# Stick-breaking attention: one scan of VectorE over two query tiles in place of one scan per tile

## The chip, the cores and the metric

The kernel runs on one core of a Trainium2 chip. The metric is device microseconds of one execution. Five engines work at once and wait for each other by semaphores: TensorE (PE; its weight loads are listed as PEld), VectorE (DVE), ScalarE (ACT), GpSimd (POOL) and SyncE (SP), whose queue issues most DMAs. Each engine runs its instructions in the program's order.

## The reference

A two-layer trunk over 2048 positions of width 1024. Layer 0 is a pooling mixer; layer 1 is attention with 16 heads of width 64. What the change touches is the attention:

```python
logits = einsum('bhtd,bhsd->bhts', q[:, :, t0:L], k[:, :, :L]) * SB_SCALE
mask = s_idx < t_idx
log_keep = where(mask, log_sigmoid(-logits), 0.0)
later = cumsum(log_keep, reverse=True) - log_keep
a = where(mask, exp(log_sigmoid(logits) + later), 0.0)
out = einsum('bhts,bhsd->bhtd', a, v[:, :, :L])
```

For a query t, key s gets beta(t,s) times the product of (1 - beta) over all keys between s and t, with beta the sigmoid of the logit. With p(s) the product of the keeps 1 - beta from key s up to t, the weight is p(s+1) - p(s), so one running product over the keys, from the newest key to the oldest, holds all that is needed. The differences are taken on V instead (rows of V are subtracted ahead of attention), and the product p itself is multiplied with them.

## The kernel before

Queries and keys are cut into 4 chunks of 512. A **slot** is one (query chunk c, head h, key chunk kc); the sweep goes over c = 3, 2, 1, 0, over the 16 heads of each, and over kc from c down to 0, 160 slots in all. A head of c=3 thus has 4 slots, of c=2 three, and so on. The slot with kc = c is the diagonal one, where query tile j (128 queries) sees only the first (j+1)*128 keys of the chunk. A slot has 4 **steps** j, one for each tile of 128 queries, 640 steps in all. In step n three things are issued, each for a different slot:

- `turn` for the slot of 6 steps ago (`LAG_T`): PE transposes one block of 128 keys of all four query tiles of the running product, up to 4 transposes (L981, PSUM tile `psa`, 2 buffers); ACT casts it to fp32r as a high part (L984), DVE subtracts that from it as a low part (L985, tile `at`). The transposes of turn n+2 reuse the PSUM buffer of turn n, so they wait for its subtraction.
- `front` for this step: two matmuls of queries and keys (L956, L957, tile `psl`), ACT's sigmoid of the negative logits, which is the keep (L960, tile `kap`, 4 buffers), and DVE's scan, the running product from the last column to the first (tile `pp`). Off the diagonal (L968) it begins at `carry`, the last value of the same query tile's scan one slot before. On the diagonal (L965) it multiplies and takes the maximum with `ahead`, which is 1 for columns that a query may not see.
- `gather` for the slot of 8 steps ago (`LAG_G`): two matmuls of V with the high and low part (L993, L994).

Between these, PE gets **dense pieces**: single matmuls of 128x512 (L1043, L1045, L1047, tile `psd`) of the gate projection and of what follows attention for the chunk that is done. `shares` spreads them over the steps: it holds a cost of DVE's work in each step (`vector`, by the widths of the scan and of the turned tile), a cost of PE's own work (`tensor`), and gives each step so many pieces that PE's time is in one proportion k to DVE's. From some steps into c=1 on, `turn` is called for two blocks at every even step (turns "by two"), and the pieces are spread evenly.

POOL has the products of the gates (L1083, L1013), the low parts of some operands (L1056, L1128) and 32 DMAs. What a slot's tiles are called and which line issues them does not depend on c.

Of the kernel before, what the change touches and what calls it, by code (L numbers as in the profile page):

```python
# [9 lines left out]
F32 = mybir.dt.float32  # L10
# [5 lines left out]
P = 128  # L16
# [19 lines left out]
def trunk_kernel(ctx, tc, x, xt, pt0, wut, cols, heads, zin, grp, aout, agate, aple,  # L36
# [851 lines left out]
    with ExitStack() as st:  # L888
        kap = st.enter_context(tc.tile_pool(name="kap", bufs=1))
        ppool = st.enter_context(tc.tile_pool(name="ppool", bufs=12))  # L890
        t2 = st.enter_context(tc.tile_pool(name="s2", bufs=2))
# [3 lines left out]

        NK = 4
        kaps = [kap.tile([P, W5], F32, name=f"kap{i}") for i in range(NK)]
        zeros = kap.tile([P, 1], F32, name="zeros")
        V.memset(zeros, 0.0)

        ahead = kap.tile([P, W5], F32, name="ahead")
        G.memset(ahead, 0.0)
        G.affine_select(out=ahead[:, W5 - P :], in_=ahead[:, W5 - P :], pattern=[[-1, P]], compare_op=ALU.is_gt,
                        fill=1.0, base=0, channel_multiplier=1)
        kcount = [0]
# [43 lines left out]
        def front(st, j):  # L949

            w = (j + 1) * P if st["diag"] else W5
            r0 = W5 - w
# [3 lines left out]
            T.matmul(ps[:, :w], qa[:, qs], kk[:, :w], start=True, stop=False)  # L956
            T.matmul(ps[:, :w], qb[:, qs], kk[:, :w], start=False, stop=True)  # L957
            kp = kaps[kcount[0] % NK]
            kcount[0] += 1
            A.activation(out=kp[:, r0:], in_=ps[:, :w], func=AF.Sigmoid, scale=-1.0)  # L960

            def scan():
                pp = ppool.tile([P, W5], F32, tag="pp", name="pp")
                if st["diag"]:
                    V.tensor_tensor_scan(out=pp[:, r0:][:, ::-1], data0=kp[:, r0:][:, ::-1],  # L965
                                         data1=ahead[:, r0:][:, ::-1], initial=1.0, op0=ALU.mult, op1=ALU.max)
                else:
                    V.tensor_tensor_scan(out=pp[:, ::-1], data0=kp[:, ::-1], data1=zeros.to_broadcast([P, W5]),  # L968
                                         initial=st["carry"][j], op0=ALU.mult, op1=ALU.add)
# [124 lines left out]
        def post(c):  # L1094
# [120 lines left out]
        def shares(n0, n1, total):  # L1215
            scan, turned_, gathered = ([widths(n, lag) for n in range(n0, n1)] for lag in (0, LAG_T, LAG_G))
# [3 lines left out]
            tensor = [2 * max(0.109, 0.2265 * a / W5) * (a > 0) + 0.109 * t / P + 2 * max(0.109, 0.2265 * g / W5) * (g > 0)  # L1220
                      for a, t, g in zip(scan, turned_, gathered)]
            part = lambda k: [max(0.5, (k * v - t) / 0.2265) + (AHEAD if n0 + i < LAG_T else 0)
# [138 lines left out]
```

## Time and profile before

| | |
|---|---|
| median of 3 runs | 2652.79 us (2652.48 to 2655.35) |
| the profiled execution | 2653.59 us, its span 2651.8 us |
| granted clock of TensorE | 1.0 |
| busy in the span: PE, PEld, DVE, ACT, POOL | 2640.3, 2205.3, 1984.8, 1427.5, 939.8 us |
| attention, from its first step to the last | about 1305 to 2536 us |
| DVE scans off the diagonal | 384 of 512 columns, mean 1337 ns |
| DVE scans on the diagonal | 64 each of 128, 256, 384, 512 columns |

Rows of a timeline have the start in us from the span's start, the busy time in us, then engine, line, operation, out<-in, shape and, in brackets, idle time of the engine just before with what ended it. Matmuls are pipelined: the next may start before the end that is given for one, so the distance of two starts tells how fast they go. Rows of groups have the count, then the busy time in us and the mean of one in ns, then the idle time before them. In rows of built programs a scan is called SCALAR_TENSOR_TENSOR.

### The profile page before, as it was taken

The numbers are of one execution on the slowest core, as the hardware profiler recorded it, in microseconds if no ns is written. First come the engines' busy times: TensorE is split into PE (matmuls) and PEld (weight loads), VectorE is DVE, ScalarE is ACT, GpSimd is POOL, SyncE is SP. The second block draws the span as 40 slices with busy tenths as digits, with TensorE's granted clock in tenths as the row PEclk, the third lists the DMA queues.
The fourth block names the chain that finished last, engine by engine and source line by source line (L and its number), as shares of the span: only waits on it lengthen the run. The fifth ranks groups of instructions, "written<-read, shape, count | busy, mean of one in ns | idle before, by whom it ended". The sixth has DMA issues, their size and how long they took to land.

```text
span 2651.8 us, 38568 instructions
## 1 busy us (share of the span) xinstructions
PE 2640.3 (100%) x13102; PEld 2205.3 (83%) x13102; DVE 1984.8 (75%) x2570; ACT 1427.5 (54%) x2767; POOL 939.8 (35%) x740
## 2 busy tenths in 40 slices
PE   9999999999999999999999999999999999999999
PEld 8888888888888888888888888888888888888887
DVE  6767835677367763767599999999999998886633
ACT  5446523556136641455466666666666666665531
POOL 2665437644485444753221111122111211212220
PEclk9999999999999999999999999999999999999999
DMA  8658885587856878447787665556766777779865
GB/s 325 227 165 302 283 314 186 191 300 253 308 177 225 301 237 304 147 153 240 229 277 229 187 215 170 175 164 194 209 200 173 190 217 238 201 209 287 248 229 178
DMA packets 469826, 600.40 MB, mean 226 GB/s; under 512 B 28607, under 2 KB 308415, under 8 KB 469629
## 3 DMA queue, kind: packets, MB, share of 16 engines
q1 hardware_dynamic: 463272, 587.39, 67.7%
q0 software_dynamic: 4608, 8.39, 2.0%
q10 hardware_dynamic: 1748, 2.17, 0.3%
q8 instruction: 103, 1.69, 0.3%
q14 instruction: 95, 0.77, 0.1%
HBM read 438.40 MB, written 153.16 MB: 223 GB/s over the span
## 4 chain that ended last, share of the span: by engine, by line
PE 89%; DMA 3%; DVE 2%; POOL 2%; ACT 2%; issue 1%; SPq 0%; ACTq 0%; DVEq 0%; POOLq 0%
PE psd L619 16%; PE psa L981 9%; PE psd L166 8%; PE psd L167 8%; PE psd L168 8%; PE psd L1043 6%; PE psd L1045 6%; PE psd L1047 6%; PE pso L994 5%; PE psl L957 5%; PE pso L993 5%; PE psl L956 5%; DMA wraw<-in_bq_dram 1%; PE psdt L1043 1%; PE psdt L1045 1%
## 5 line engine op out<-in xcount | busy, mean ns | idle before, releaser
L619 PE MATMUL psd<-wpair,x 128*128 128x512 f32 x2304 | 525.6, 390 | 1.4 <-DVE wpair L149 0.8
L968 DVE TENSOR_TENSOR_SCAN pp<-kap,pp,zeros 128x512 f32<-128x512 f32 x384 | 512.7, 1337 | 7.8 <-ACT kap L960 7.1
L984 ACT CAST at<-psa 128x512 fp32r<-128x512 f32 (+3 forms) x640 | 325.7, 523 | 348.8 <-PE psa L981 337.8
L619 PEld LDWEIGHTS psd<-wpair,x 128*128 128x128 f32 x2304 | 431.7, 188 | 93.0 <-DVE wpair L149 2.2
L985 DVE TENSOR_TENSOR at<-psa,at 128x512 fp32r<-128x512 f32 (+3 forms) x640 | 374.9, 598 | 62.2 <-ACT at L984 57.7
L960 ACT ACTIVATE kap<-psl 128x512 f32<-128x512 f32 (+3 forms) x640 | 345.7, 540 | 93.9 <-PE psl L957 90.4
L981 PE MATMUL psa<-ident,pp 128*128 128x128 f32 x2176 | 329.4, 273 | 2.3 <-DVE at L985 1.5
L981 PEld LDWEIGHTS psa<-ident,pp 128*128 128x128 f32 x2176 | 263.7, 141 | 58.4 <-DVE at L985 4.2
L956 PE MATMUL psl<-kk,qa 128*128 128x512 f32 (+3 forms) x640 | 275.1, 430 | 0.2 <-DMA kk<-kd 0.2
L965 DVE TENSOR_TENSOR_SCAN pp<-kap,ahead 128x128 f32<-128x128 f32 (+3 forms) x256 | 224.2, 877 | 40.2 <-ACT kap L960 38.8
L994 PE MATMUL pso<-at,vv 128*128 128x512 f32 (+3 forms) x640 | 234.0, 366 | 0.0
L957 PE MATMUL psl<-kk,qb 128*128 128x512 f32 (+3 forms) x640 | 232.9, 364 | 0.0
L993 PE MATMUL pso<-at,vv 128*128 128x512 f32 (+3 forms) x640 | 232.2, 363 | 0.0
L167 PE MATMUL psd<-xp,wpair 128*128 128x512 f32 x512 | 199.5, 390 | 1.4 <-DVE xp L320 1.4
L166 PE MATMUL psd<-xp,wpair 128*128 128x512 f32 x512 | 200.1, 391 | 0.7 <-ACT xp L319 0.7
L168 PE MATMUL psd<-xp,wpair 128*128 128x512 f32 x512 | 199.3, 390 | 0.0
L149 DVE SCALAR_TENSOR_TENSOR wpair<-wraw,gains,wpair 128x512 fp32r<-128x512 f32 x192 | 164.8, 891 | 31.9 <-ACT wpair L148 30.9
L143 POOL TENSOR_TENSOR wpair<-wraw,wpair 128x512 fp32r<-128x512 f32 x99 | 145.1, 1475 | 78.9 <-ACT wpair L141 72.2
L148 ACT ACTIVATE wpair<-wraw,gains 128x512 fp32r<-128x512 f32 x192 | 129.7, 716 | 47.4 <-DMA wraw<-in_bq_dram 35.6
L1083 POOL TENSOR_TENSOR zr<-zr,sgz 128x512 f32<-128x512 f32 x32 | 61.4, 1919 | 263.8 <-ACT sgz L1082 236.6
L141 ACT CAST wpair<-wraw 128x512 fp32r<-128x512 f32 x148 | 89.1, 618 | 104.5 <-PE psd L168 61.1
L994 PEld LDWEIGHTS pso<-at,vv 128*128 128x128 f32 x640 | 120.3, 188 | 26.4
(206 smaller groups left out, 5400.4 us busy)
## 6 DMA issues: line engine op xcount, KB each, us to landing
kk<-kd SPq DMA_DIRECT2D x160, 256.0 KB
vv<-vd SPq DMA_DIRECT2D x160, 256.0 KB
wraw<-in_kv_dram SPq DMA_DIRECT2D x128, 256.0 KB
wpair<-wzd SPq DMA_DIRECT2D x64, 512.0 KB
wpair<-wod SPq DMA_DIRECT2D x64, 512.0 KB
wpair<-wgd SPq DMA_DIRECT2D x64, 512.0 KB
wpair<-wu SPq DMA_DIRECT2D x48, 512.0 KB
wpair<-wi SPq DMA_DIRECT2D x36, 512.0 KB
```

Source lines behind the costliest of these rows:

```text
L166: T.matmul(ps, wst(units, kt, 0, c0), acts[kt][:, 0], start=(begin and kt == order[0]), stop=False)
L167: T.matmul(ps, wst(units, kt, 0, c0), acts[kt][:, 1], start=False, stop=False)
L168: T.matmul(ps, wst(units, kt, 1, c0), acts[kt][:, 0], start=False, stop=(end and kt == order[-1]))
L619: T.matmul(pss2[i], ck["x2"][kt][:, xh, tk], wst(ws, kt, wh, 0, W5), start=(kt == 0 and xh == 0 and wh == 0), stop=(kt == KT - 1 and wh == 1))
L956: T.matmul(ps[:, :w], qa[:, qs], kk[:, :w], start=True, stop=False)
L957: T.matmul(ps[:, :w], qb[:, qs], kk[:, :w], start=False, stop=True)
L960: A.activation(out=kp[:, r0:], in_=ps[:, :w], func=AF.Sigmoid, scale=-1.0)
L968: V.tensor_tensor_scan(out=pp[:, ::-1], data0=kp[:, ::-1], data1=zeros.to_broadcast([P, W5]), initial=st["carry"][j], op0=ALU.mult, op1=AL ...
L981: T.transpose(pt[:, j * P : (j + 1) * P], pp[:, r0 + kt * P : r0 + (kt + 1) * P], ident)
L985: V.tensor_tensor(out=at[:, 1, cs], in0=pt[:, cs], in1=f(at[:, 0, cs]), op=ALU.subtract)
L993: T.matmul(po[:, cs], vv[:, kt, :], at[:, 0, cs], start=(st["diag"] and kt == 0), stop=False)
L994: T.matmul(po[:, cs], vv[:, kt, :], at[:, 1, cs], start=False, stop=(st["last"] and kt == 3))
```

## The change

Tiles j = 0, 1 and j = 2, 3 of a slot now share one scan. Their keeps stand beside each other in one tile of 1025 columns: the odd tile in columns up to 511, the even one from 513, and column 512 between them holds a keep of 0, so that the product begins anew there from what the second operand has in that column. Off the diagonal the second operand is `entry`, zeros with one column into which POOL copies the odd tile's carry. On the diagonal it is `ahead`, two constant tiles with a 1 in that column. The scan is issued in the odd steps alone. The keeps have 2 buffers in place of 4, the products 5 of 1025 columns in place of 12 of 512. `shares` gets new costs for the scan and the mean width of the two tiles of a pair. A tile `ple` of the dense part moves to another pool.

```diff
+        TWO = 2 * W5 + 1
+        kaps = [kap.tile([P, TWO], F32, name=f"kap{i}") for i in range(2)]
+        entry = kap.tile([P, TWO + W5 + 1], F32, name="entry")
+        firsts = [entry[:, i * (W5 + 1) : i * (W5 + 1) + TWO] for i in range(2)]
+        for t in (*kaps, entry):
+            V.memset(t, 0.0)
+        ahead = []
+        for i in range(2):
+            w = (2 * i + 1) * P
+            d = kap.tile([P, W5 + 1 + w], F32, name=f"ahead{i}")
+            V.memset(d, 0.0)
+            G.memset(d[:, W5 : W5 + 1], 1.0)
+            for at in (W5 - P, W5 + 1 + w - P):
+                G.affine_select(out=d[:, at : at + P], in_=d[:, at : at + P], pattern=[[-1, P]], compare_op=ALU.is_gt,
+                                fill=1.0, base=0, channel_multiplier=1)
+            ahead.append(d)
...
-            kp = kaps[kcount[0] % NK]
-            kcount[0] += 1
-            A.activation(out=kp[:, r0:], in_=ps[:, :w], func=AF.Sigmoid, scale=-1.0)
+            if not j % 2:
+                kcount[0] += 1
+            kp, first = kaps[kcount[0] % 2], firsts[kcount[0] % 2]
+            r0 = W5 - w if j % 2 else W5 + 1
+            A.activation(out=kp[:, r0 : r0 + w], in_=ps[:, :w], func=AF.Sigmoid, scale=-1.0)
+            if not j % 2:
+                if not st["diag"]:
+                    G.tensor_copy(out=first[:, W5 : W5 + 1], in_=st["carry"][j + 1])
+                return lambda: None
             def scan():
-                pp = ppool.tile([P, W5], F32, tag="pp", name="pp")
+                pp = ppool.tile([P, TWO], F32, tag="pp", name="pp")
+                both = slice(r0, W5 + 1 + (w - P if st["diag"] else W5))
                 if st["diag"]:
-                    V.tensor_tensor_scan(out=pp[:, r0:][:, ::-1], data0=kp[:, r0:][:, ::-1],
-                                         data1=ahead[:, r0:][:, ::-1], initial=1.0, op0=ALU.mult, op1=ALU.max)
+                    V.tensor_tensor_scan(out=pp[:, both][:, ::-1], data0=kp[:, both][:, ::-1],
+                                         data1=ahead[j // 2][:, both][:, ::-1], initial=1.0, op0=ALU.mult, op1=ALU.max)
                 else:
-                    V.tensor_tensor_scan(out=pp[:, ::-1], data0=kp[:, ::-1], data1=zeros.to_broadcast([P, W5]),
-                                         initial=st["carry"][j], op0=ALU.mult, op1=ALU.add)
-                st["carry"][j] = pp[:, r0 : r0 + 1]
-                st["a"].append((pp, r0))
+                    V.tensor_tensor_scan(out=pp[:, both][:, ::-1], data0=kp[:, both][:, ::-1], data1=first[:, both][:, ::-1],
+                                         initial=st["carry"][j - 1], op0=ALU.mult, op1=ALU.add)
+                for i, at in ((j - 1, W5 + 1), (j, r0)):
+                    st["carry"][i] = pp[:, at : at + 1]
+                    st["a"].append((pp, at))
...
-                pr = t2.tile([P, 2, W5], F32R, tag="ple", name="ple")
+                pr = pair("ple")
...
-            vector = [(0.15 + 0.0022 * a if a else 0.0) + (0.14 + 0.00105 * t if t else 0.0) for a, t in zip(scan, turned_)]
+            scan = [(widths(n // 2 * 2, 0) + widths(n // 2 * 2 + 1, 0)) / 2 for n in range(n0, n1)]
+            vector = [(0.1 + 0.00208 * a if a else 0.0) + (0.14 + 0.00105 * t if t else 0.0) for a, t in zip(scan, turned_)]
```

What this does to the order of the instructions, first on DVE, at the end of the eleventh head of c=3 and the first steps of the next (the diagonal ones, with `ahead`). Before:

```order
L968 SCALAR_TENSOR_TENSOR pp<-kap_12081,pp,zeros 128x512
L985 TENSOR_TENSOR at<-psa,at 128x512
L968 SCALAR_TENSOR_TENSOR pp<-kap_12082,pp,zeros 128x512
L985 TENSOR_TENSOR at<-psa,at 128x512
L968 SCALAR_TENSOR_TENSOR pp<-kap_12083,pp,zeros 128x512
L985 TENSOR_TENSOR at<-psa,at 128x512
L965 SCALAR_TENSOR_TENSOR pp<-kap_12080,ahead 128x128
```

One subtraction stood between two scans. The same place in the changed program, where the lines of these instructions are L1000, L982 and L979:

```order
L982 SCALAR_TENSOR_TENSOR pp<-kap_12081,pp,entry 128x1025
L1000 TENSOR_TENSOR at<-psa,at 128x512 x2
L982 SCALAR_TENSOR_TENSOR pp<-kap_12080,pp,entry 128x1025
L1000 TENSOR_TENSOR at<-psa,at 128x512 x2
L979 SCALAR_TENSOR_TENSOR pp<-kap_12081,ahead_12086 128x385
```

Now two subtractions stand between two scans, and the first of them stands behind a scan of both tiles. On PE the order of kinds is as before, and only the dense pieces sit elsewhere. The first diagonal steps of that next head, from the matmuls of its 128 keys to the transposes two steps on, before:

```order
L956 MATMUL psl<-kk,qa 128x128
L957 MATMUL psl<-kk,qb 128x128
L993 MATMUL pso<-at,vv 128x512
L994 MATMUL pso<-at,vv 128x512
L981 MATMUL psa<-ident,pp 128x128 x4
L956 MATMUL psl<-kk,qa 128x256
L957 MATMUL psl<-kk,qb 128x256
L1047 MATMUL psd<-xz,wpair 128x512
L993 MATMUL pso<-at,vv 128x512
L994 MATMUL pso<-at,vv 128x512
L981 MATMUL psa<-ident,pp 128x128 x4
```

And now (L963 and L964 are the matmuls of queries and keys, L996 the transposes, L1008 and L1009 those with V, L1062 a dense piece):

```order
L963 MATMUL psl<-kk,qa 128x128
L964 MATMUL psl<-kk,qb 128x128
L1062 MATMUL psd<-xz,wpair 128x512
L1008 MATMUL pso<-at,vv 128x512
L1009 MATMUL pso<-at,vv 128x512
L996 MATMUL psa<-ident,pp 128x128 x4
L963 MATMUL psl<-kk,qa 128x256
L964 MATMUL psl<-kk,qb 128x256
L1008 MATMUL pso<-at,vv 128x512
L1009 MATMUL pso<-at,vv 128x512
L996 MATMUL psa<-ident,pp 128x128 x4
```

The piece has moved one step up; the step ahead of these rows had three pieces before and has two now, so that three pieces in place of four lie between that step's matmuls and the last transposes shown.

More of the change, by code (lines that the diff above doesn't have):

```diff
@@ L894, in trunk_kernel @@
         psl = st.enter_context(tc.tile_pool(name="psl", bufs=2, space=bass.MemoryType.PSUM))
[L896 to L904, printed above, removed]
+        TWO = 2 * W5 + 1
[14 more added lines that the diff above has]
+            ahead.append(d)
         kcount = [0]
@@ L1215, in shares @@
         def shares(n0, n1, total):
-            scan, turned_, gathered = ([widths(n, lag) for n in range(n0, n1)] for lag in (0, LAG_T, LAG_G))
-            vector = [(0.15 + 0.0022 * a if a else 0.0) + (0.14 + 0.00105 * t if t else 0.0) for a, t in zip(scan, turned_)]
+            front_, turned_, gathered = ([widths(n, lag) for n in range(n0, n1)] for lag in (0, LAG_T, LAG_G))
+            scan = [(widths(n // 2 * 2, 0) + widths(n // 2 * 2 + 1, 0)) / 2 for n in range(n0, n1)]
+            vector = [(0.1 + 0.00208 * a if a else 0.0) + (0.14 + 0.00105 * t if t else 0.0) for a, t in zip(scan, turned_)]
             for k in range(len(early["v"])):
@@ L1220, in shares @@
             tensor = [2 * max(0.109, 0.2265 * a / W5) * (a > 0) + 0.109 * t / P + 2 * max(0.109, 0.2265 * g / W5) * (g > 0)
-                      for a, t, g in zip(scan, turned_, gathered)]
+                      for a, t, g in zip(front_, turned_, gathered)]
             part = lambda k: [max(0.5, (k * v - t) / 0.2265) + (AHEAD if n0 + i < LAG_T else 0)
```

3 lines of the change are left out of this document (1 added, 2 removed).

## The prediction

> **What bounds the kernel now.** I read the stretches of the attention part first, then the timeline where one head ends and the next begins, then the page's groups. Columns of the first view: stretch, its length, then busy time of PE, PEld, DVE, ACT, POOL, granted clock, DMA share, GB/s.
>
> ```profile
> 1305.00:1775.00 470.00, 468.63 (x2589) 392.47 (x2588) 452.45 (x537) 304.46 (x605) 80.46 (x50) 1.00 0.67 205
> 1775.00:2127.00 352.00, 351.15 (x1950) 294.81 (x1949) 337.38 (x407) 235.51 (x482) 71.74 (x47) 1.00 0.67 191
> 2127.00:2374.00 247.00, 246.72 (x1370) 210.41 (x1369) 216.49 (x281) 157.66 (x345) 46.69 (x33) 1.00 0.75 216
> sum 1231.00, PE 1228.43 PEld 1035.50 DVE 1109.06 ACT 784.09 POOL 239.52; mean PE 307.11 PEld 258.87 DVE 277.26 ACT 196.02 POOL 59.88
> ```
>
> The rows are the sweeps of query chunks c=3, c=2 and c=1; the sum takes c=0 in too. PE is idle for 1231.00-1228.43 = 2.6 us of 1231. DVE is 96% busy in the first two, so both look full. Which one sets the pace shows in the timeline, here the last step of a head of c=3 and the first three of the next head. Its diagonal steps have 128, 256, 384 columns, so PE passes them fast.
>
> ```profile
> 1625.83 0.39 PE L957 MATMUL psl<-kk,qb 128*128 128x512 f32 x1
> 1627.22 0.60 PE L981 MATMUL psa<-ident,pp 128*128 128x128 f32 x4
> 1627.33 1.66 DVE L968 TENSOR_TENSOR_SCAN pp<-kap,pp,zeros 128x512 f32<-128x512 f32 x1
> 1627.89 0.39 PE L957 MATMUL psl<-kk,qb 128*128 128x512 f32 x1
> 1629.50 1.27 DVE L968 TENSOR_TENSOR_SCAN pp<-kap,pp,zeros 128x512 f32<-128x512 f32 x1
> 1629.73 0.39 PE L957 MATMUL psl<-kk,qb 128*128 128x512 f32 x1
> 1629.75 0.59 ACT L984 CAST at<-psa 128x512 fp32r<-128x512 f32 x1 [0.75 <-PE psa L981]
> 1629.96 0.40 PE L1047 MATMUL psd<-xz,wpair 128*128 128x512 f32 x1
> 1630.19 0.40 PE L1043 MATMUL psd<-xz,wpair 128*128 128x512 f32 x1
> 1630.23 0.60 ACT L960 ACTIVATE kap<-psl 128x512 f32<-128x512 f32 x1
> 1630.43 0.39 PE L1045 MATMUL psd<-xz,wpair 128*128 128x512 f32 x1
> 1630.69 0.66 DVE L985 TENSOR_TENSOR at<-psa,at 128x512 fp32r<-128x512 f32 x1
> 1631.28 1.27 DVE L968 TENSOR_TENSOR_SCAN pp<-kap,pp,zeros 128x512 f32<-128x512 f32 x1
> 1632.47 0.66 DVE L985 TENSOR_TENSOR at<-psa,at 128x512 fp32r<-128x512 f32 x1
> 1633.62 0.60 PE L981 MATMUL psa<-ident,pp 128*128 128x128 f32 x4
> ```
>
> A matmul of 512 columns is issued every 0.23 us (1629.73, 1629.96, 1630.19, 1630.43), and no gap follows. PE runs at its issue rate and DVE just keeps up: the subtraction L985 ends at 1633.13, and the transposes that reuse its PSUM buffer start at 1633.62. That 0.49 us is the margin here. PE's work is the bound, and the only thing to win is its 2.6 us of idle time.
>
> By the Trainium skill (Trainium Kernel Development and Optimization, section Performance Expectations), a matmul busy time says little and the share of weight loads says more. That share is 392.47/470 = 83%; by the rule alone, 17% would be open. In the dense part ahead of attention, where no other engine is waited for, it reads
>
> ```profile
> L619 PE MATMUL psd<-wpair,x 128*128 128x512 f32 x2304 | 525.6, 390 | 1.4 <-DVE wpair L149 0.8
> L619 PEld LDWEIGHTS psd<-wpair,x 128*128 128x128 f32 x2304 | 431.7, 188 | 93.0 <-DVE wpair L149 2.2
> ```
>
> that is 431.7/525.6 = 82%. So 83% is full here; the rule only keeps a chance for the second rival.
>
> **What the change takes from DVE.**
>
> ```profile
> L968 DVE TENSOR_TENSOR_SCAN pp<-kap,pp,zeros 128x512 f32<-128x512 f32 x384 | 512.7, 1337 | 7.8 <-ACT kap L960 7.1
> 1604.18 0.41 DVE L965 TENSOR_TENSOR_SCAN pp<-kap,ahead 128x128 f32<-128x128 f32 x1
> 1605.53 0.68 DVE L965 TENSOR_TENSOR_SCAN pp<-kap,ahead 128x256 f32<-128x256 f32 x1
> 1607.53 0.95 DVE L965 TENSOR_TENSOR_SCAN pp<-kap,ahead 128x384 f32<-128x384 f32 x1
> 1608.97 1.21 DVE L965 TENSOR_TENSOR_SCAN pp<-kap,ahead 128x512 f32<-128x512 f32 x1
> ```
>
> Slope (1.21-0.41)/384 = 2.083 ns a column; fixed part 0.41-128*0.002083 = 0.14 us; 1.27-1.21 = 0.06 more for an initial value from SBUF. A joined scan of 1025 columns was never run: 2.14+0.14+0.06 = 2.34 us. Bounds: 2.14 (columns alone) and 2*1.337 = 2.67 (two of today's mean). I take 2.34, since the slope holds over four widths. It replaces 2*1.27, so 0.20 less, 192 times: 38 us. On the diagonal 385 columns cost 0.94 and 897 2.01 in place of 0.41+0.68 and 0.95+1.21: 0.15 less, 128 times: 19 us. DVE loses 57 us of work, and as DVE is not the bound, this shortens nothing but the 2.6 us in which PE waits.
>
> **What it adds off the path.**
>
> ```profile
> L683 DVE MEMSET vs<- 1x512 f32 x2 | 1.0, 485 | 0.2 <-DVE vv L709 0.2
> L507 POOL COPY work<-halo 128x16 f32<-128x16 f32 x32 | 10.0, 314 | 12.2 <-DVE hl L744 11.5 <-DVE halo L235 0.7
> 1305.55 0.06 DVE L899 MEMSET zeros<- 128x1 f32 x1 [13.20 <-PE psl L956]
> 1317.05 0.60 PE L981 MATMUL psa<-ident,pp 128*128 128x128 f32 x4
> ```
>
> Five fills of 5126 columns in all, at 485 ns for 512: 4.9 us on DVE from 1305.55 on, so about to 1310.5; POOL's four triangles follow. The first sigmoid waits for the first two fills, the first scans for the triangles. The first transposes come at 1317.05 and PE has dense matmuls until then, so the 6 us left cover two scans of 0.94 and 2.01. Cost 0; without that cover it would be 5 us. POOL gets 192 copies of one column, 0.31 us each (nearest row, 16 columns): 60 us on an engine busy 80 of 470 us. A copy can run when the scan of the slot before has ended, four steps of about 1.84 us ahead of the next, so 7.3-2.3 = 5 us of cover against 0.31 plus whatever POOL has in hand. Zero, with a rival below. What waits for the copy is the scan, behind it the subtractions, and PE for those. PE's instructions are the same in number. The tile ple moves into the pool of pairs, whose 18 buffers then hold og, x3 and ple (8+8+2) of one chunk, so none is asked back while it is read: 0.
>
> **What it adds on the path.** Today DVE works on the even tile while PE makes the odd one. Now the scan starts when the odd sigmoid is done, and the subtraction of the next step stands behind all of it. At the head shown: sigmoid done 1630.83. No scan at 1629.50 is ahead of the subtraction, so this runs from its cast's end (1629.75+0.59 = 1630.34) to 1631.0; the joined scan starts about 1630.96 and ends 1633.30. The next subtraction overlaps it by 0.08 (1632.47 against 1631.28+1.27) and ends 0.66 later, at 1633.88. PE takes it 0.05 later, as this row pair of before shows where PE did wait:
>
> ```profile
> 1863.21 0.66 DVE L985 TENSOR_TENSOR at<-psa,at 128x512 fp32r<-128x512 f32 x1
> 1863.92 0.66 PE L981 MATMUL psa<-ident,pp 128*128 128x128 f32 x4 [0.15 <-DVE at L985]
> ```
>
> So the transposes can start at 1633.93, 4.20 us after the odd tile's L957 at 1629.73, while PE comes there after 3.89 us today, and after 3.66 at this head once the new filling has moved a dense piece of 0.23 away from it. PE waits 0.31 or 0.54 us, and behind it stand all its later matmuls. In the middle of a head a step takes 2.06 or 1.84 us (L957 at 1625.83, 1627.89, 1629.73). Three of them less the 0.65 from transposes to L957 (1627.22 to 1627.89) leave about 5 us, and nothing waits. In c=2 and at the start of c=1, where dense pieces are still lacking, the same place reads:
>
> ```profile
> 1905.62 0.39 PE L957 MATMUL psl<-kk,qb 128*128 128x512 f32 x1
> 1909.70 0.60 PE L981 MATMUL psa<-ident,pp 128*128 128x128 f32 x4
> 2140.59 0.40 PE L957 MATMUL psl<-kk,qb 128*128 128x512 f32 x1
> 2144.07 0.60 PE L981 MATMUL psa<-ident,pp 128*128 128x128 f32 x4
> ```
>
> That is 4.08 and 3.48 us. The sum, with the pieces counted in the new order: c=3 has 15 such heads, 9 with four pieces on the way (0.28 each, as a mean of 0.25 to 0.31) and 6 with three (0.52): 5.6 us. c=2 has 16: 10 unmoved (0.13) and 6 with a piece less (0.37): 3.5. c=1 has 2 before turns go by two; the subtraction is narrower there, 0.41 in place of 0.68 by the rows below, so 0.5 to 0.7, taken as 0.6: 1.2. At 4 heads the new order puts one more DVE operation, 0.67 less 0.08 of overlap, between scan and subtraction: 2.4.
>
> ```profile
> L985 DVE TENSOR_TENSOR at<-psa,at 128x512 fp32r<-128x512 f32 x448 | 301.7, 679 | 51.3 <-ACT at L984 47.2
> L985 DVE TENSOR_TENSOR at<-psa,at 128x256 fp32r<-128x256 f32 x64 | 26.0, 406 | 9.4 <-ACT at L984 9.1
> L1077 DVE TENSOR_TENSOR zr<-psd,rb 128x512 f32<-128x512 f32 x32 | 21.4, 668 | 0.1
> ```
>
> Together 12.7. Of the 2.6 us of PE's idle time I take half as won: -1.3. Net +11.4 on the profiled execution's 2653.6 (span 2651.8, 1.8 around it), which is 0.8 over the median. Forecast 2664 us for the median.
>
> Its own range comes from the scan's bounds. At 2.14 each wait is 0.20 shorter: 9*0.08+6*0.32, 6*0.17, 2*0.4 and 4*0.4 give 6, less at most 2.6: +3.4, 2656. At 2.67 they are 0.33 longer: 9*0.61+6*0.85, 10*0.46+6*0.70, 1.9 and 2.4 give 24: 2677.
>
> **Rivals.**
> *No change to be measured.* The waits shrink to a few us since the scan costs its columns alone and a lighter DVE never lags: +3.4 at most by the sum above, 0 if the subtractions run earlier than I place them. For it: DVE's load falls by 57 of 1109 us. Against: the wait needs no backlog, only the scan's length. 2650 to 2657.
> *Faster, DVE as the bound.* Were DVE's 96% the pace of c=3 and c=2, their 160 joined scans and 64 diagonal ones would give 160*0.20+64*0.15 = 42 us: 2611. Against it: matmuls every 0.23 us and 2 us of idle time in 822.
> *Much slower, through POOL.* This row shows what a copy can stand behind:
>
> ```profile
> 1609.08 2.19 POOL L1083 TENSOR_TENSOR zr<-zr,sgz 128x512 f32<-128x512 f32 x1 [15.90 <-ACT sgz L1082]
> ```
>
> It began as the 1.21 us scan at 1608.97 ran, and the scan at 1627.33 took 1.66 beside another such: the two engines hold each other up. One POOL operation (2.19), a joined scan (2.34) and the copy (0.31) make 4.84 of the 5 us. It decides from two POOL operations ahead on: then the scan starts 2.0 us late and PE loses about 1.5. With one copy in five it is 38*1.5 = 57 us: 2710. Against: POOL is 17% busy. The Trainium skill (SBUF — State Buffer, section SBUF: two separate sides) has a lock on a shared port, held for the whole instruction, between GpSimd and a Vector operation with two SBUF inputs. By it the loser waits for all of the other's operation; the trace shows +0.39 on that scan, less than the rest of the POOL operation, so it bears it out in part.
>
> **Numbers.** Forecast 0.64, no change 0.25, DVE 0.05, POOL 0.06. 0.2% is 5.3 us, about what can be told from no change here. So slower 0.70, same 0.25, faster 0.05. The range 2651 to 2677 holds the forecast's own 2656 to 2677 and nearly all of the second case.
>
> **What would show it.** Right: joined scans of about 2.3 us, DVE's busy time some 50 us lower, PE's idle time up by about 10 us, put down to DVE's subtraction at the transposes, once per head in c=3 and c=2, hardly any elsewhere; POOL's copies done before their scans. Wrong: a scan far from 2.34; idle PE spread over all steps, or ended by POOL; transposes at the heads starting 3.7 us after L957.

## The result, and the profile after

| | before | after |
|---|---|---|
| median, the two side by side (6 runs each) | 2654.17 us | 2674.16 us |
| lowest to highest | 2652.48 to 2655.35 | 2673.84 to 2676.29 |
| ratio, with its 95% interval | | 1.0078, 1.0065 to 1.0091 |
| profiled execution; its span | 2653.59; 2651.8 us | 2674.06; 2672.3 us |
| DVE busy in the span | 1984.8 us | 1930.7 us |

The changed kernel is 0.8% slower, some 20 us, although DVE has 54 us less to do. The same stretches of attention as in the prediction, now of the changed kernel (length, then busy time of PE, PEld, DVE, ACT, POOL, granted clock, DMA share, GB/s):

```profile
1305.00:1775.00 470.00, 462.12 (x2536) 383.23 (x2535) 424.38 (x405) 297.01 (x593) 104.77 (x147) 1.00 0.66 202
1775.00:2127.00 352.00, 344.15 (x1900) 286.10 (x1899) 309.54 (x303) 228.66 (x466) 81.18 (x106) 1.00 0.64 185
2127.00:2374.00 247.00, 244.70 (x1353) 207.65 (x1353) 206.50 (x216) 158.54 (x345) 52.79 (x67) 1.00 0.74 214
```

The stretches are fixed in time, so the second now begins with the last 9 us of c=3. The granted clock is 1.00 in all three, as before. PE was busy for 468.63 and 351.15 us in the first two stretches before; it is now idle for 8 us in each. The first matmul of attention starts at 1304.51 (before 1305.32), so the dense part ahead of it lost nothing. By the starts of the first matmul of each chunk, c=3 takes 479.9 us (470.6 before), c=2 362.0 (351.6), c=1 248.6 (246.8), the rest, up to the last transpose, 173.4 (173.2): 9.3, 10.4, 1.8 and 0.2 us more.

Who ends PE's idle time, from the groups of waits (engine, line, waited for: us in total, times, longest), first before, then after:

```profile
PEld psa L981 <- DVE at L985: 4.2, 9, 0.9
```

```profile
PE psa L996 <- DVE at L1000: 17.9, 33, 1.5
PEld psa L996 <- DVE at L1000: 35.4, 45, 1.7
```

It is the wait of the transposes for DVE's subtraction of the low part. A wait can be listed under PE, under PEld or under both, so I use one measure for all kernels below: the distance from the matmul ahead to the first transpose, less what that distance is when nothing is waited for (0.23 us behind a matmul of 512 columns), summed where over 0.04 us. This gives **3.8 us in the kernel before and 24.9 in the changed one**. The difference of 21.1 accounts for the whole loss (20.5 us between the profiled executions). At the 33 head ends that the prediction names stand 17.7 of the 24.9.

The groups of the changed kernel, by form:

```profile
L982 DVE TENSOR_TENSOR_SCAN pp<-kap,pp,entry 128x1025 f32<-128x1025 f32 x192 | 458.3, 2387 | 33.3 <-ACT kap L969 29.2 <-POOL entry L972 0.9 <-POOL x L1143 0.5
L979 DVE TENSOR_TENSOR_SCAN pp<-kap,ahead 128x897 f32<-128x897 f32 x64 | 130.6, 2041 | 32.0 <-ACT kap L969 31.4 <-POOL ahead L910 0.4
L979 DVE TENSOR_TENSOR_SCAN pp<-kap,ahead 128x385 f32<-128x385 f32 x64 | 67.3, 1052 | 16.7 <-ACT kap L969 16.5
```

The median joined scan takes 2.346 us, the diagonal ones 2.018 and 0.955. DVE's idle time before the joined scans is put down to ACT's sigmoid of the odd tile (29.2 of 33.3 us), hardly to POOL's copy (0.9): DVE waits for the odd tile, and then all of the scan is still to be done.

A head end as the prediction drew it, in the timeline of the changed kernel (start, duration; the last step of a head of c=3 and two short diagonal ones):

```profile
1545.11 0.39 PE L964 MATMUL psl<-kk,qb 128*128 128x512 f32 x1
1545.61 0.60 ACT L969 ACTIVATE kap<-psl 128x512 f32<-128x512 f32 x1
1545.74 0.69 DVE L1000 TENSOR_TENSOR at<-psa,at 128x512 fp32r<-128x512 f32 x1 [0.36 <-ACT at L999]
1546.35 2.35 DVE L982 TENSOR_TENSOR_SCAN pp<-kap,pp,entry 128x1025 f32<-128x1025 f32 x1
1548.61 1.26 DVE L1000 TENSOR_TENSOR at<-psa,at 128x512 fp32r<-128x512 f32 x2
1548.76 0.39 PE L1009 MATMUL pso<-at,vv 128*128 128x512 f32 x1
1549.33 0.66 PE L996 MATMUL psa<-ident,pp 128*128 128x128 f32 x4 [0.18 <-DVE at L1000]
1549.74 0.42 PE L963 MATMUL psl<-kk,qa 128*128 128x384 f32 x1
```

The sigmoid is done at 1546.21, the joined scan starts at 1546.35, the first of the two subtractions behind it ends near 1549.28, and the transposes start at 1549.33: 4.22 us after L964. PE started its last matmul at 1548.76 and could have gone on 0.23 later. It stood still for 0.33 us, and everything behind it on PE is that much later. Part of that wait is listed at PEld, so the row shows only 0.18.

### The profile page after: what moved, and what is told of

Same layout as the page of the kernel before. It is cut to its first block, busy times and chain, and to the rows that moved or that the text cites. A ratio compares the mean times of both kernels' runs of the same rounds, so it can differ in the third digit from the quotient of the medians.

```text
span 2672.3 us, 38837 instructions
## 1 busy us (share of the span) xinstructions
PE 2645.4 (99%) x13102; PEld 2202.3 (82%) x13102; DVE 1930.7 (72%) x2254; ACT 1429.9 (54%) x2767; POOL 991.7 (37%) x936
## 4 chain that ended last, share of the span: by engine, by line
PE 87%; DVE 4%; issue 3%; ACT 2%; POOL 2%; DMA 2%; SPq 0%; ACTq 0%; DVEq 0%; POOLq 0%
PE psd L619 16%; PE psd L167 8%; PE psd L166 8%; PE psa L996 8%; PE psd L168 8%; PE psd L1058 6%; PE psd L1060 6%; PE psd L1062 6%; PE psl L964 4%; PE psl L963 4%; PE pso L1009 4%; PE pso L1008 4%; DVE at L1000 1%; DVE pp L982 1%; PE psdt L1058 1%
## 5 line engine op out<-in xcount | busy, mean ns | idle before, releaser
L982 DVE TENSOR_TENSOR_SCAN pp<-kap,pp,entry 128x1025 f32<-128x1025 f32 x192 | 458.3, 2387 | 33.3 <-ACT kap L969 29.2
L1000 DVE TENSOR_TENSOR at<-psa,at 128x512 fp32r<-128x512 f32 (+3 forms) x640 | 371.1, 599 | 97.4 <-ACT at L999 94.5
L996 PE MATMUL psa<-ident,pp 128*128 128x128 f32 x2176 | 331.5, 274 | 18.1 <-DVE at L1000 17.9
L996 PEld LDWEIGHTS psa<-ident,pp 128*128 128x128 f32 x2176 | 261.0, 140 | 83.4 <-DVE at L1000 35.4
L972 POOL COPY entry<-pp 128x1 f32<-128x1 f32 x192 | 44.5, 232 | 629.5 <-DVE pp L979 385.9
L963 PE MATMUL psl<-kk,qa 128*128 128x512 f32 (+3 forms) x640 | 275.4, 430 | 0.0
L1009 PE MATMUL pso<-at,vv 128*128 128x512 f32 (+3 forms) x640 | 233.8, 366 | 0.0
L979 DVE TENSOR_TENSOR_SCAN pp<-kap,ahead 128x385 f32<-128x385 f32 (+1 forms) x128 | 198.0, 1547 | 48.7 <-ACT kap L969 48.0
L964 PE MATMUL psl<-kk,qb 128*128 128x512 f32 (+3 forms) x640 | 233.1, 364 | 0.0
L1008 PE MATMUL pso<-at,vv 128*128 128x512 f32 (+3 forms) x640 | 231.1, 361 | 0.0
L148 ACT ACTIVATE wpair<-wraw,gains 128x512 fp32r<-128x512 f32 x192 | 130.0, 718 | 44.2 <-DMA wraw<-in_bq_dram 32.6
L1009 PEld LDWEIGHTS pso<-at,vv 128*128 128x128 f32 x640 | 120.2, 188 | 25.9
```

Source lines behind the costliest of these rows:

```text
L982: V.tensor_tensor_scan(out=pp[:, both][:, ::-1], data0=kp[:, both][:, ::-1], data1=first[:, both][:, ::-1], initial=st["carry"][j - 1], op ...
L996: T.transpose(pt[:, j * P : (j + 1) * P], pp[:, r0 + kt * P : r0 + (kt + 1) * P], ident)
L1000: V.tensor_tensor(out=at[:, 1, cs], in0=pt[:, cs], in1=f(at[:, 0, cs]), op=ALU.subtract)
L1008: T.matmul(po[:, cs], vv[:, kt, :], at[:, 0, cs], start=(st["diag"] and kt == 0), stop=False)
L1009: T.matmul(po[:, cs], vv[:, kt, :], at[:, 1, cs], start=False, stop=(st["last"] and kt == 3))
```

## The experiments

Each ratio is to the kernel before on the same chip and stands with its interval; the waits are PE's before the transposes, by the measure above, in the one profiled execution of each kernel.

| kernel | median us | ratio (95%) | waits us | of them at the 33 head ends |
|---|---|---|---|---|
| before | 2652.79 | | 3.8 | 0.4 |
| changed | 2674.16 | 1.0078 (1.0065 to 1.0091) | 24.9 | 17.7 |
| own_steps | 2651.04 | 0.9991 (0.9982 to 1.0001) | 3.6 | 1.3 |
| both_odd | 2698.22 | 1.0168 (1.0153 to 1.0183) | 44.2 | 29.5 |
| head_fill | 2660.82 | 1.0028 (1.0017 to 1.0039) | 11.7 | 3.4 |
| old_fill | 2669.78 | 1.0067 (1.0052 to 1.0082) | 20.8 | 14.8 |
| new_fill_before | 2651.87 | 0.9996 (0.9987 to 1.0006) | 3.3 | 1.1 |
| heads_split | 2666.68 | 1.0050 (1.0035 to 1.0065) | 16.9 | 8.6 |
| slot_split | 2665.06 | 1.0047 (1.0032 to 1.0062) | 13.9 | 5.8 |
| two_slots_split | 2659.97 | 1.0028 (1.0017 to 1.0038) | 10.4 | 4.7 |
| last_joined | 2666.04 | 1.0050 (1.0036 to 1.0064) | 16.6 | 13.3 |
| copies_twice | 2672.88 | 1.0079 (1.0064 to 1.0094) | 24.3 | 17.3 |
| no_gate | 2671.09 | 1.0071 (1.0054 to 1.0088) | 21.7 | 15.6 |
| own_fill | 2650.75 | 0.9991 (0.9982 to 1.0000) | 2.9 | 0.2 |

In every row the time above the kernel before (ratio less 1, times 2652.8) is the waits less 3.8 to within 2.4 us (4.2 in both_odd). So the waits at the transposes account for the loss.

**own_steps** keeps the changed kernel's tiles, fills and shares, and undoes the joining alone: each tile has a scan of its own, in its own step. POOL's copies fall away with it. The word `own` in the code stands for the tile's own step; in both_odd, below, it is `odd`.

```diff
+            split = True
+            pick = (lambda: ahead[j // 2]) if st["diag"] else (lambda: first)
...
+            def one(i, at, n, first_of=None):
+                cs = slice(at, at + n)
+                V.tensor_tensor_scan(out=st["pp"][:, cs][:, ::-1], data0=kp[:, cs][:, ::-1], data1=pick()[:, cs][:, ::-1],
+                                     initial=1.0 if st["diag"] else st["carry"][i], op0=ALU.mult,
+                                     op1=ALU.max if st["diag"] else ALU.add)
...
             if not j % 2:
-                if not st["diag"]:
+                if not st["diag"] and not split:
                     G.tensor_copy(out=first[:, W5 : W5 + 1], in_=st["carry"][j + 1])
-                return lambda: None
...
+                def even():
+                    st["pp"] = ppool.tile([P, TWO], F32, tag="pp", name="pp")
+                    one(j, W5 + 1, w)
...
+                return even if split and 'own' == "own" else (lambda: None)
```

> The changed kernel with its tiles, its buffers and its filling of dense pieces, but each query tile has a scan of its own again, issued in its own step, and POOL copies no carry. Theory (PE waits where a head ends because the subtraction stands behind a scan that begins only after the odd sigmoid): the waits at the heads, 17.7 us in the trace of the changed kernel, go, and the time returns to that of before, 2654 within 4. Rival (the new filling, the smaller number of buffers or the moved tile cost the time): it stays at 2668 to 2676. Rival (POOL's copies or the joined instruction): back to 2654 too; this run alone does not tell that one from the theory, the next does.

Measured: 0.9991, and 3.6 us of waits. All of the loss is gone, so the constants, the buffers, the tile ple and the new shares cost nothing that can be told.

**both_odd** is own_steps with both scans issued in the odd step; the even one takes two more columns. Nothing is joined, nothing copied, but the start is as late as in the changed kernel.

```diff
+                if split:
+                    if 'odd' == "odd":
+                        st["pp"] = ppool.tile([P, TWO], F32, tag="pp", name="pp")
+                        one(j - 1, W5 - 1, 2 + (w - P if st["diag"] else W5), W5 + 1)
+                    one(j, r0, w)
+                    return
```

> As the run own_steps, but the even tile's scan takes two more columns, one of them written by the odd tile's sigmoid, so that both scans stand one behind the other after the odd sigmoid. No joined scan, no copies. Theory: the late start is what costs. Two scans take 2*1.27 less 0.08 of overlap = 2.46 us in place of 2.35, so from the odd tile's L964 to the transposes a clean head needs 4.34 us in place of 4.23; 33 heads wait 0.11 longer and a slower DVE lags more: 2678 to 2690. Rival (the joined instruction itself or POOL's copies): 2654 to 2660.

Measured: 1.0168, more than the theory had. Its wait of PE for the subtraction:

```profile
PE psa L1019 <- DVE at L1023: 34.6, 53, 1.8
```

A pair of scans at the end of a head of c=3 in both_odd:

```profile
1434.23 2.60 DVE L975 TENSOR_TENSOR_SCAN pp<-kap,pp,entry 128x514 f32<-128x514 f32 x2
```

At the heads of c=3 and c=2 the last scan ahead of the subtraction ends 4.11 us (median) after L964, 3.60 in the changed kernel and 2.73 in own_steps; the transposes follow at 4.75, 4.23 and 3.89. The pair takes 2.60 us (also the median), where the expectation had 2.46: the second scan starts 0.04 us after the first has ended, where it was expected 0.08 us before that end. Both write one column of the tile, which would explain it but was not tested, so a part of the excess may be this edit's own. The late start, without a joined scan or a copy, is enough to bring the whole loss; the joined scan at 2.35 us is shorter than the pair.

**head_fill** is the changed kernel with at least two dense pieces in each of the first two steps of a diagonal slot, so that PE has more to do where the wait was forecast.

```diff
+            least = lambda n: 2.0 if n // 4 < len(slots) and slots[n // 4][2] == slots[n // 4][0] and n % 4 < 2 else 0.5
-            part = lambda k: [max(0.5, (k * v - t) / 0.2265) + (AHEAD if n0 + i < LAG_T else 0)
+            part = lambda k: [max(least(n0 + i), (k * v - t) / 0.2265) + (AHEAD if n0 + i < LAG_T else 0)
```

> The changed kernel with all its joined scans, but the filling gives each of the first two steps of a diagonal slot at least 2 dense pieces (in c=3 and c=2), taken from the other steps; PE's work is the same. From the odd tile's L964 to the transposes lie 7 to 8 pieces in place of 3 to 6, 0.5 to 0.9 us more of PE's work. Theory: the waits of clean heads (0.13 to 0.56) vanish, of those that lag (0.64 to 1.18) a part stays, some 3 us in all; elsewhere the slack is 0.8 us and shrinks by less: 2657 to 2663. Rival (joined scans or copies): 2672 to 2676, as PE's total work and DVE's are unchanged.

Measured: 1.0028, so 13 of 20 us are back with the joined scan untouched. The same head as above, in head_fill's timeline:

```profile
1543.41 0.40 PE L964 MATMUL psl<-kk,qb 128*128 128x512 f32 x1
1544.66 2.34 DVE L982 TENSOR_TENSOR_SCAN pp<-kap,pp,entry 128x1025 f32<-128x1025 f32 x1
1545.41 0.44 PE L1060 MATMUL psd<-xz,wpair 128*128 128x512 f32 x1
1545.69 0.40 PE L1062 MATMUL psd<-xz,wpair 128*128 128x512 f32 x1
1546.92 1.47 DVE L1000 TENSOR_TENSOR at<-psa,at 128x512 fp32r<-128x512 f32 x2
1547.99 0.60 PE L996 MATMUL psa<-ident,pp 128*128 128x128 f32 x4
```

The scan and the subtractions stand as before the edit. Two pieces now lie in the first diagonal step, PE comes to the transposes 4.58 us after L964, and it finds the subtraction done (near 4.18) and waits for nothing.

**old_fill** and **new_fill_before** take the shares apart from the rest. old_fill is the changed kernel with the costs of before and each step's own width:

```diff
-            vector = [(0.1 + 0.00208 * a if a else 0.0) + (0.14 + 0.00105 * t if t else 0.0) for a, t in zip(scan, turned_)]
+            vector = [(0.15 + 0.0022 * a if a else 0.0) + (0.14 + 0.00105 * t if t else 0.0) for a, t in zip(front_, turned_)]
```

> As the changed kernel, but the shares of dense pieces are worked out with the costs of the kernel before, so that a piece goes back between the last L964 of a head and the transposes at the 12 heads where the changed fill moved it away. By the prediction's sum each of these waits is 0.23 us shorter: 2.8 us, so 2670 to 2673 us. If the fill has no part: 2673 to 2676 us. If the changed fill were most of the loss: 2655 to 2662 us.

Measured: 1.0067. By the time alone it can't be told from the changed kernel's 1.0078, since the intervals overlap; in the traces the waits at the heads fall from 17.7 to 14.8 us, 2.9 against the 2.8 expected. new_fill_before is the reverse edit on the kernel before:

```diff
+            scan = [(widths(n // 2 * 2, 0) + widths(n // 2 * 2 + 1, 0)) / 2 for n in range(n0, n1)]
-            vector = [(0.15 + 0.0022 * a if a else 0.0) + (0.14 + 0.00105 * t if t else 0.0) for a, t in zip(scan, turned_)]
+            vector = [(0.1 + 0.00208 * a if a else 0.0) + (0.14 + 0.00105 * t if t else 0.0) for a, t in zip(scan, turned_)]
```

> The kernel before with the costs and mean widths of the changed shares alone, nothing else changed. PE has 0.49 us of margin at a head, and the fill takes 0.23 of it at 12 heads: 2651 to 2656 us, a ratio of 0.9985 to 1.0015. If the fill by itself made PE wait, 2657 or more.

Measured: 0.9996. The new shares harm only where the margin is already used up.

**heads_split** gives tiles 2 and 3 of the last slot of a head their own scans again, and **slot_split** all four tiles of that slot; both leave the rest joined.

```diff
-            split = True
+            split = st["last"] and not st["diag"] and j >= 2
```

> The changed kernel, in which only the last pair of tiles of each head off the diagonal (key chunk 0, tiles 2 and 3; 48 of the 192 pairs) has two scans in two steps again; all others are joined. Theory: the waits at the 33 heads (17.7 us) go and what waits elsewhere (7.1 us) stays: 2657 within 4. Rival (POOL's copies or the joined scans wherever they stand): a quarter of the loss at most, 2668 to 2671.

```diff
-            split = True
+            split = st["last"] and not st["diag"]
```

> As the changed kernel, but in the off-diagonal slots of key chunk 0 (the last slot of each head) both pairs have a scan for each tile in its own step; all other slots keep the joined scan. If the late joined scans of the head's last slot are the cause (both of them, since the one of tiles 0 and 1 has already put the scan of tile 2 behind), PE's waits go back to about 4 to 9 us and the time is 2656 to 2661 us. If the joined scans of the diagonal slot that follows are as much to blame, the waits stay at about 12 to 17 us and the time at 2663 to 2668 us, as with tiles 2 and 3 alone split (2666.7). If joining costs the same wherever it stands, 32 to 35 of the 320 pairs' worth are won and the time is 2670 us or more.

Measured: 1.0050 and 1.0047. The theory missed both: it had 2653 to 2661 us, and 13.9 us of waits were left with no joined scan at all in the last slot. The timeline of slot_split shows why, from the joined scan of the slot before, over the first own scan, to the transposes behind the head:

```profile
1478.86 2.35 DVE L1005 TENSOR_TENSOR_SCAN pp<-kap,pp,entry 128x1025 f32<-128x1025 f32 x1
1479.14 3.16 POOL L1121 TENSOR_TENSOR zr<-zr,sgz 128x512 f32<-128x512 f32 x1 [4.78 <-ACT sgz L1120]
1479.93 0.61 ACT L969 ACTIVATE kap<-psl 128x512 f32<-128x512 f32 x1
1481.70 1.68 DVE L975 TENSOR_TENSOR_SCAN pp<-kap,pp,entry 128x512 f32<-128x512 f32 x1
1485.65 0.60 ACT L969 ACTIVATE kap<-psl 128x512 f32<-128x512 f32 x1
1487.44 1.27 DVE L975 TENSOR_TENSOR_SCAN pp<-kap,pp,entry 128x512 f32<-128x512 f32 x1
1488.63 1.26 DVE L1023 TENSOR_TENSOR at<-psa,at 128x512 fp32r<-128x512 f32 x2
1489.34 0.44 PE L1019 MATMUL psa<-ident,pp 128*128 128x128 f32 x2
```

The first sigmoid is done at 1480.54, but DVE is in the joined scan until 1481.21 and has a subtraction to do; the own scan starts 1.16 us after the sigmoid. Three steps on the lag is still 1487.44 - 1486.25 = 1.19. In this head a product of POOL adds to it (the first own scan takes 1.68 us in place of 1.27); over all heads of c=3 the median goes from 1.18 at the first own scan of the slot to 0.93 at the last. With own scans a step has 1.27 and 0.66 us of work for DVE, less 0.08 of overlap, and PE passes a step in 1.84 to 2.06: DVE has next to no time to catch up in. The mean lag of the last scan of these heads behind its sigmoid is 0.96 us in slot_split and 0.44 in the kernel before. What the subtraction stands behind is the end of that scan. As a mean over the 32 heads of c=3 and c=2 it comes 1.74 us after the sigmoid in the kernel before, 2.23 in slot_split and 2.65 in the changed kernel. Undoing the join in this slot thus wins back 0.42 us, less than half of the way; at 31 heads that is 13 us, and the waits at the heads fell by 11.9 (17.7 to 5.8). In the other kernels the two go together as well: 2.38 us and 8.6 us of waits in heads_split, 2.52 and 13.3 in last_joined (below), 3.17 and 29.5 in both_odd.

**two_slots_split** was to test that: own scans in the last two off-diagonal slots, so that the inherited lag has four more steps to go.

```diff
-            split = True
+            split = st["kc"] < 2 and not st["diag"]
```

> As the changed kernel, but in the off-diagonal slots of key chunks 0 and 1 (the last two slots of each head) every tile has its own scan in its own step. With the last slot alone split (1.0047), own scans started 1.1 to 1.2 us after their sigmoid at its first step and still 0.9 at its last, where the kernel before has 0.4: they inherit the delay from the joined scan one slot before and win back 0.07 to 0.11 us a step. If that is why the waits stayed, four more steps win back 0.3 to 0.45 us: at the last step the lag is about 0.45 us in c=3 and 0.7 in c=2, PE's waits fall from 13.9 to some 7 to 9 us, and the ratio is 1.002 to 1.0035 (2658 to 2661 us). If the waits came from the joined scans of the diagonal slot behind the head, which are as they were, the ratio stays at 1.004 to 1.0055.

Measured: 1.0028, as the inherited lag had it and not as the diagonal slot behind had it. But the forecast of the lag itself was wrong for c=3: it is 0.88 us (median) at the last step, where 0.45 was expected, and 0.69 in c=2 against 0.7. The mean over both is 0.85, 0.11 less than in slot_split, which at 31 heads would be 3.4 us. The waits at the heads fell by 1.1 us only (5.8 to 4.7); the other 2.4 of the 3.5 us went elsewhere. PE's waits, 10.4 us, missed the 7 to 9 expected, so the time fell into its range without its working holding. So lag and waits go down together, but a lag does not decay at a steady rate per step, and what decides its decay stays open.

**last_joined** is the opposite cut: own scans throughout, and only the 48 pairs of tiles 2 and 3 in the last off-diagonal slots joined.

```diff
-            split = True
+            split = not (st["last"] and not st["diag"] and j >= 2)
```

> The opposite cut: every tile has its own scan in its own step, and only tiles 2 and 3 of the slot of key chunk 0 of each head (48 of 320 pairs) keep the joined scan. If what counts is when the joined scan at the end of a head starts and ends against the transposes behind it, these 48 alone bring most of the loss back: 31 heads of c=3 and c=2 at some 0.4 to 0.55 us each, 2 of c=1 at 0.6, so 14 to 18 us, a ratio of 1.0045 to 1.0075 (2664 to 2672 us). If the loss is spread over all joined scans, 48 of 320 of 20 us are 3 us: a ratio below 1.003 (under 2660 us).

Measured: 1.0050. 15% of the pairs bring 13 of the 20 us, as the theory of the place had it and not as a cost spread over all pairs had it (3 us). Here DVE comes to the joined scan without a backlog from earlier ones:

```profile
L1005 DVE TENSOR_TENSOR_SCAN pp<-kap,pp,entry 128x1025 f32<-128x1025 f32 x48 | 112.7, 2347 | 18.5 <-ACT kap L969 16.4 <-POOL x L1166 1.6 <-POOL zr L1121 0.2
```

None is stretched (the mean is 2347 ns), DVE stands idle before them, and the waits at the heads are 13.3 us; the prediction's sum for them was 12.7.

**copies_twice** does POOL's copy of the carry twice.

```diff
                     G.tensor_copy(out=first[:, W5 : W5 + 1], in_=st["carry"][j + 1])
+                    G.tensor_copy(out=first[:, W5 : W5 + 1], in_=st["carry"][j + 1])
```

> As the changed kernel, but POOL copies each odd tile's carry into the second operand twice, so 192 copies of 0.23 us more, half of them in the way of other POOL work and all of them ahead of their scan. By the theory they are hidden: 2673 to 2677 us. If the copies hold scans up, each second copy moves those scans 0.2 us further, 10 to 35 us in all: 2684 to 2710 us.

Measured: 1.0079 against 1.0078. The copies are hidden.

**no_gate** leaves POOL's 32 products of the gate with its sigmoid out.

```diff
-                    G.tensor_tensor(out=zr, in0=zr, in1=sg, op=ALU.mult)
```

> As the changed kernel, but POOL's 32 products of the gate with its sigmoid (128x512, 2.2 us each) are left out, so the gate's value enters without its sigmoid. By the theory that the late start is the main cause and POOL only stretches a few scans, about 3 to 7 us of PE's waits go and the time is 2667 to 2671 us. If POOL's products were the main cause, through stretched scans and copies that stand behind them, 12 us or more go: 2662 us or less. If POOL had no part: 2673 to 2676 us.

Measured: 1.0071. The time is not to be told from the changed kernel's; in the trace 3.2 us of waits are gone (24.9 to 21.7). POOL is a small part of it, not the cause.

**own_fill** is own_steps with head_fill's two pieces, as a try for a kernel that beats both.

```diff
+            split = True
...
-            part = lambda k: [max(0.5, (k * v - t) / 0.2265) + (AHEAD if n0 + i < LAG_T else 0)
+            part = lambda k: [max(least(n0 + i), (k * v - t) / 0.2265) + (AHEAD if n0 + i < LAG_T else 0)
```

> Own scans in their own steps (all tiles), with the changed tiles and fill, and at least two dense pieces in the first two steps of each diagonal slot. If own scans leave PE 2.6 to 4 us of idle time and nothing else is to be won, it is 2648 to 2654 us, a ratio of 0.9975 to 1.0005: not to be told from own scans without the two pieces. If the few us that own scans seemed to gain (0.9991) come from the fill, it goes below 2648.

Measured: 0.9991, interval 0.9982 to 1.0000, against 0.9991 for own_steps. The 1.8 to 2.5 us are at the edge of what can be measured, and the two pieces add nothing to be seen. Nothing here is shown to beat the kernel before.

## Why the prediction was right, and what it mis-sized

Direction, place and mechanism held. The size was 11.4 us forecast and 20 measured, inside the range. That the range held it is in part luck: its upper end, 2677, stands for a joined scan of 2.67 us. The scan took 2.35, as forecast, and with that the sum had nothing that reaches 2674; what makes up the difference is below, and the length of an undisturbed scan is no part of it.

- **PE as the bound.** Held. DVE lost 54 of the 57 us of work forecast, and own_fill, without waits at the heads, is within 0.2% of before: there was nothing to win. DVE's share of c=3 fell from 96% to 424.38/470 = 90% while the time went up, and head_fill, with the same lighter DVE and 3.4 us of waits at the heads, is still 0.28% above before. So the rival with DVE as the bound (2611) is out.
- **The joined scan at 2.34 us.** 2.346 measured, and 2.018 and 0.955 for 2.01 and 0.94. The mean of 2.387 has the scans that ran beside POOL in it. The 0.06 us in it that the prediction put down to the initial value from SBUF is there in own_steps too, with a whole tile as second operand in both cases (median 1.275 us off the diagonal, 1.216 on it, for 512 columns); as the operation differs too, the cause of it is not shown.
- **4.20 us from L957 (now L964) to the transposes.** Held where nothing else disturbs: 4.23 us at the median, and waits of 0.32 to 0.34 or 0.55 us in c=3 (0.28 and 0.52 as means forecast), 0.13 to 0.16 or 0.38 to 0.39 in c=2 (0.13 and 0.37).
- **An added operation at 4 heads.** Held. One of them:

```profile
1663.77 0.39 PE L964 MATMUL psl<-kk,qb 128*128 128x512 f32 x1
1665.02 2.35 DVE L982 TENSOR_TENSOR_SCAN pp<-kap,pp,entry 128x1025 f32<-128x1025 f32 x1
1667.28 0.67 DVE L1092 TENSOR_TENSOR zr<-psd,rb 128x512 f32<-128x512 f32 x1
1667.86 0.68 DVE L1000 TENSOR_TENSOR at<-psa,at 128x512 fp32r<-128x512 f32 x1
1668.60 0.66 PE L996 MATMUL psa<-ident,pp 128*128 128x128 f32 x4 [0.79 <-DVE at L1000]
```

  4.83 us from L964, so 0.60 more than without it, where 0.59 was forecast.
- **The sum at the heads, 12.7.** This was mis-sized: 17.7 measured. It priced each head as if only the scan's length counted. At ten heads something comes on top, worked out head by head against a plain one: at six DVE comes to the scan 0.1 to 2.0 us late (about 2.0 us of waits), at two the scan is stretched beside POOL (about 1.3), at two the odd sigmoid itself is late (about 0.7). That is some 4 of the 5.0; the rest is up to 0.09 us more than forecast at each of the other heads. A head with the stretched scan:

```profile
1873.15 0.39 PE L964 MATMUL psl<-kk,qb 128*128 128x512 f32 x1
1874.06 1.27 POOL L1098 TENSOR_TENSOR zr<-zr,sgz 128x512 f32<-128x512 f32 x1
1874.40 3.08 DVE L982 TENSOR_TENSOR_SCAN pp<-kap,pp,entry 128x1025 f32<-128x1025 f32 x1
1878.12 0.66 PE L996 MATMUL psa<-ident,pp 128*128 128x128 f32 x4 [0.96 <-DVE at L1000]
```

- **"hardly any elsewhere", and half of PE's idle time won: -1.3.** This failed. Away from the heads PE now waits 7.2 us, and by the same measure it waited 3.8 in all before. The lighter DVE did not take waits away. own_steps, which undoes the joining alone, has 2.3 us there, so the joined scans bring the other 4.9. The likely reason is that DVE has its work in longer pieces, so that whatever comes late finds a scan of 2.35 us ahead of it in place of one of 1.27; no run tests that place by place. With 5.0 from the heads, these 3.4 + 1.3 make up the 9.7 between the 21.1 of waits and the forecast's 11.4.
- **Zero for the fills, the copies and ple.** Held. The five fills take 4.5 us where 4.9 were forecast, attention starts no later, a copy takes 0.23 us where 0.31 was taken (its row, of the changed kernel), and twice the copies cost nothing.

```profile
L972 POOL COPY entry<-pp 128x1 f32<-128x1 f32 x192 | 44.5, 232 | 629.5 <-DVE pp L979 385.9 <-DVE pp L982 239.8 <-DMA qa<-qd 3.7
```

  The idle 629.5 us before the copies are POOL waiting for the scans that make the carries, not the other way round.
- **No change to be measured** (0.25) fell on its point: the scan does not cost its columns alone.
- **Much slower, through POOL** (2710) fell with copies_twice and no_gate. What was right in it is that the two engines hold each other up; that is worth some 3 us here.

## What to carry to other kernels

Joining two operations saves their fixed time on the engine, but the joined one starts when the later input is there and gives nothing back until all of it is done. Before joining, take the shortest stretch of work that the bounding engine has between the instruction that makes the later input (here L964) and the next thing that it needs from this engine, and compare it with the joined operation and everything queued behind it; here it was 3.7 to 4.1 us against 4.2, at 31 of the 64 head ends. An engine that is 96% busy hands a delay on from step to step, so undoing the join just at the place of the wait brings back only part of the loss; giving the bounding engine something to do there (head_fill) brought back most of it.

## What the runs showed of the hardware

**VectorE's scan and GpSimd's products exclude each other**, far more strictly than the prediction had it. From the timeline of the changed kernel, in turn: a scan, a product of POOL that begins within it, the next product, and a scan that begins within that:

```profile
1517.14 2.34 DVE L982 TENSOR_TENSOR_SCAN pp<-kap,pp,entry 128x1025 f32<-128x1025 f32 x1
1518.03 2.53 POOL L1098 TENSOR_TENSOR zr<-zr,sgz 128x512 f32<-128x512 f32 x1 [6.40 <-ACT sgz L1097]
1520.53 1.29 POOL L1028 TENSOR_TENSOR os<-os,zt 128x512 f32<-128x512 f32 x1
1520.59 2.05 DVE L979 TENSOR_TENSOR_SCAN pp<-kap,ahead 128x385 f32<-128x385 f32 x1
```

The first scan is not stretched; the product ends 1.08 us after it, almost its own 1.29. The second scan takes 1.10 us more than its 0.95, and the product ahead had 1.23 left. Of the scans that begin inside one product of POOL and see no other, 34 in all, those with over 0.3 us of it left are longer by what is left less 0.13 to 0.20 us; of 54 products that begin inside a scan, 49 end 1.07 to 1.11 us after it, and two that met a scan itself held up ran at once. Whichever starts first runs undisturbed and the other waits for it to end. The Trainium skill (SBUF — State Buffer, section SBUF: two separate sides) has just this, a lock held for the whole instruction between GpSimd and a Vector operation with two SBUF inputs, and the trace agrees. The prediction held the scan of 1.66 us at 1627.33 against it. The row of POOL beside it, in the kernel before:

```profile
1625.80 2.12 POOL L1083 TENSOR_TENSOR zr<-zr,sgz 128x512 f32<-128x512 f32 x1 [4.78 <-ACT sgz L1082]
```

The scan was 0.39 us longer, and POOL's row still had 0.59; with the 0.20 at the end of a POOL row that does not count, the two are equal. So a joined scan of 2.35 us also locks POOL out for longer at a time: the 32 products (L1083, now L1098) take 2.19 us on average in the changed kernel and 1.92 in the kernel before.

**The scan's price.** 2.083 ns a column held from 128 to 1025 columns (0.955, 2.018 and 2.346 us measured at 385, 897 and 1025 columns, 0.94, 2.01 and 2.34 worked out with it). The Trainium skill (DVE: opcode table, instruction layouts, handler registers and perf-mode slots, section 6. Datapath and trigger behaviour) has the scan at half throughput; no run here shows a full rate to set beside it.
